# A two-layer mixer block on Trainium2: the feed-forward part in two phases, with seven half-size products in place of eight on the way up

## The chip, the cores and the metric

The kernel runs on one core of one Trainium2 chip. The figure is the device time of one execution in microseconds (us); the median of 3 runs of the kernel before is 4048.8 us (4048.6 to 4054.81). All work is done by five engines with instruction queues of their own: TensorE (PE, the matmuls; PEld is its loading of weights), VectorE (DVE), ScalarE (ACT), GpSimd (POOL) and SyncE (SP), which here issues every DMA. Each queue is worked off in order: an instruction that waits holds up all that stand behind it.

## The reference

Two layers work on 1024 tokens `x` and 256 context tokens `ctx` of 1024 channels. Each layer has three mixers side by side (a recurrent one, a gated delta rule, a Fourier one), an output projection, and then the part that the change touches:

```python
def sq_relu_mlp(h, w1, w2):
    a = jax.nn.relu(h @ w1)
    return (a * a) @ w2

for l in range(DEPTH):
    ...
    xl = xl + m[:, 2] * yx
    hx = modulate(rmsnorm(xl, norm2_g[l]), m[:, 3], m[:, 4])
    xl = xl + m[:, 5] * sq_relu_mlp(hx, mlp_w1[l], mlp_w2[l])
    # the same for the context, except in the last layer
```

`w1` is 1024 x 4096 and `w2` is 4096 x 1024, all in float32. A final norm follows.

## The kernel before, in words

Channels lie on the partitions (8 blocks of 128), tokens along the free axis. The tokens are in three pieces: A and B with 512 tokens each, and C with the 256 of the context. C is worked in layer 0 only. The residual stream of a piece is `xr`, kept in SBUF.

Every float32 product is made of three: an operand is split into a rounded high part and a low part that is the rest, and `mm3` (L293) adds high by high, high by low and low by high. ACT makes the high part of a weight (L249), POOL subtracts to get the low part (`wsplit`, L276, L289). Each matmul takes 128 input channels to 128 output channels for 512 tokens (256 for C).

The feed-forward part (`mlp`, L1491) goes through the 4096 inner channels in 16 passes of two blocks of 128. In a pass the upward product of each block takes 8 input blocks, so 24 matmuls for each of A, C and B; ACT makes the squared relu and its high part, DVE the low part (L1507). These stay in SBUF (`mhA`, `mhB`, `mhC`) and go at once into the downward product: for each of 8 output blocks, 6 matmuls (2 inner blocks by 3) and then one addition into `xr` on DVE (`residual`, L1481, L1485). A pass of layer 1 thus has 96 upward and 96 downward matmuls.

Ahead of it, at the end of `mixers` (L1740 to L1752), the output projection adds into `xr`, `rstat` (L480) gets the inverse norm of each token, and `norm` (L507) makes the high and low parts `xh` and `xl` of the normalised, modulated tokens: `spread` (L256) brings the inverse norm to all partitions by four 128 x 128 PE transposes, DVE multiplies (L526), ACT adds the shift and rounds, and DVE (L533) or POOL (L530) subtracts. This is done for A and C while PE is busy with the output projection of B; the norm of B comes last, while PE multiplies A and C.

Eight PSUM banks take the products: six for this part (ring `d`), two for small things. While layer 0's feed-forward part runs, `mod_part` streams 24 MB of `w_mod` for layer 1 and reduces it on ACT, DVE (L457) and POOL (L460). The framework lays out each engine's queue ahead of time: instructions of different steps stand interleaved where their inputs were expected to be ready.

## Time and profile before

| what | value |
|---|---|
| median of 3 runs | 4048.8 us |
| the profiled execution, its own time | 4053.91 us |
| its span, from the first to the last instruction | 4052.1 us |
| mean granted TensorE clock | 0.913 of full speed |
| PE busy | 3665.3 us (90%) |
| DVE, ACT, POOL busy | 57%, 35%, 29% |
| feed-forward part of layer 0 on PE | 1322 to about 2230 us |
| feed-forward part of layer 1 on PE | 3324 to about 4030 us |
| DMA over the span | 421.93 MB, mean 104 GB/s |

How to read it: the shares are means over stages with different limits, so the rows below are taken from the two feed-forward stages and from their starts. A matmul's recorded duration overlaps that of the next; what one costs in a full stream is the stretch of time over the number of matmuls in it. The chain of waits puts 55% of the span on the line of the matmuls (L252).

### The profile page before, as it was taken

The page shows a single profiled execution, that of the slowest core. Times are in us where ns is not written, and L with a number is a line of the kernel's source. Part 1 is how long each engine was busy: PE and PEld are TensorE (multiplying, and loading weights), DVE is VectorE, ACT ScalarE, POOL GpSimd, SP SyncE. Part 2 cuts the span into 40 slices and gives each one's busy share as a digit, 9 for nine tenths or more (in the row PEclk, how much of TensorE's full clock was granted, in tenths as well). Part 3 has the DMA queues.
Part 4 walks back from the last instruction along what each step waited for, and adds up shares of the span by engine and source line. Part 5 has one row for each costly group of instructions (what it writes and reads, how often), then busy time and mean ns, then how long its engine had stood idle before and what let it go on. Part 6 is the DMA issues. An engine that isn't in the chain of part 4 may idle for free.

```text
span 4052.1 us, 60608 instructions
## 1 busy us (share of the span) xinstructions
PE 3665.3 (90%) x24030; PEld 3077.3 (76%) x24030; DVE 2321.2 (57%) x3872; ACT 1405.0 (35%) x2571; POOL 1162.0 (29%) x870
## 2 busy tenths in 40 slices
PE   7998996886788999999999889987698889999999
PEld 5776885775677888888888766876687678888887
DVE  5646877888764544443444555658878653333334
ACT  5433443333334432222223433333333333222222
POOL 1323444332225323122111332114233233222221
PEclk8998887877888999999999899987788899999999
DMA  6334336542464212222122233246254441111111
GB/s 217 116 125 143 114 109 186 151 144 90 123 205 114 71 55 71 63 73 77 59 68 79 69 130 132 76 136 179 87 154 136 136 120 55 45 49 53 45 48 63
DMA packets 441726, 421.93 MB, mean 104 GB/s; under 512 B 28502, under 2 KB 351586, under 8 KB 441442
## 3 DMA queue, kind: packets, MB, share of 16 engines
q1 hardware_dynamic: 441442, 418.05, 33.6%
q8 instruction: 189, 3.10, 0.3%
q14 instruction: 95, 0.78, 0.1%
HBM read 324.20 MB, written 93.75 MB: 103 GB/s over the span
## 4 chain that ended last, share of the span: by engine, by line
PE 56%; DVE 8%; DMA 3%; issue 2%; ACT 2%; POOL 2%; SPq 0%; DVEq 0%; POOLq 0%; ACTq 0%
PE bank L252 55%; DMA wmod<-in_w_mod_dram 1%; DVE iD L785 1%; DVE iE L786 1%; DMA yin<-y 1%; DVE iD L779 1%; POOL wlo L289 1%; SPq L259 0%; PE bank L1145 0%; DVE macc L457 0%; PE bank L256 0%; POOL ras L1103 0%; DVE nt L272 0%; ACT whi L249 0%; DMA rvr<-rv 0%
## 5 line engine op out<-in xcount | busy, mean ns | idle before, releaser
L289 POOL TENSOR_TENSOR wlo<-wraw,whi 128x512 fp32r<-128x512 f32 x472 | 626.2, 1348 | 1731.3 <-ACT whi L249 825.7
L249 ACT ACTIVATE whi<-wraw 128x512 fp32r<-128x512 f32 x472 | 287.4, 625 | 639.4 <-PE bank L252 391.3
L252 PE MATMUL bank<-xhA,whi 128*128 128x512 f32 (+1 forms) x928 | 378.4, 408 | 0.0
L252 PE MATMUL bank<-xhB,whi 128*128 128x512 f32 (+1 forms) x928 | 365.1, 394 | 12.4 <-ACT ru L249 12.1
L252 PE MATMUL bank<-xlA,whi 128*128 128x512 f32 (+1 forms) x928 | 374.3, 404 | 1.3 <-POOL xlA L530 1.0
L252 PE MATMUL bank<-xhA,wlo 128*128 128x512 f32 (+1 forms) x928 | 372.3, 402 | 1.5 <-POOL wlo L289 1.5
L252 PE MATMUL bank<-xlB,whi 128*128 128x512 f32 (+1 forms) x928 | 365.2, 394 | 1.8 <-POOL xlB L530 1.8
L252 PE MATMUL bank<-xhB,wlo 128*128 128x512 f32 (+1 forms) x928 | 364.1, 392 | 0.0
L1485 DVE SCALAR_TENSOR_TENSOR xrB<-bank,mod,xrB 128x512 f32<-128x512 f32 x272 | 203.6, 749 | 197.2 <-PE bank L252 197.2
L252 PE MATMUL bank<-mhB,whi 128*128 128x512 f32 x1024 | 316.1, 390 | 0.0
L252 PE MATMUL bank<-mhA,whi 128*128 128x512 f32 x1024 | 315.2, 389 | 0.0
L249 ACT ACTIVATE mt<-bank 128x512 f32<-128x512 f32 (+1 forms) x160 | 88.1, 551 | 531.9 <-PE bank L252 498.0
L1485 DVE SCALAR_TENSOR_TENSOR xrA<-bank,mod,xrA 128x512 f32<-128x512 f32 x272 | 196.8, 746 | 120.3 <-PE bank L252 119.9
L252 PEld LDWEIGHTS bank<-mhA,whi 128*128 128x128 f32 x1024 | 192.2, 188 | 39.8
L252 PEld LDWEIGHTS bank<-mhB,whi 128*128 128x128 f32 x1024 | 191.1, 188 | 38.7
L252 PEld LDWEIGHTS bank<-xhA,whi 128*128 128x128 f32 (+1 forms) x928 | 179.0, 193 | 43.9 <-issue 6.2
L252 PEld LDWEIGHTS bank<-xhB,whi 128*128 128x128 f32 (+1 forms) x928 | 174.8, 188 | 49.4 <-ACT ru L249 12.5
L252 PEld LDWEIGHTS bank<-xhA,wlo 128*128 128x128 f32 (+1 forms) x928 | 178.7, 193 | 43.9 <-POOL wlo L289 2.4
L252 PEld LDWEIGHTS bank<-xlA,whi 128*128 128x128 f32 (+1 forms) x928 | 179.2, 193 | 42.8 <-POOL xlA L530 2.9
L1507 DVE TENSOR_TENSOR mhA<-mt,mhA 128x512 fp32r<-128x512 f32 x64 | 53.7, 839 | 274.7 <-ACT mt L249 274.6
L457 DVE SCALAR_TENSOR_TENSOR macc<-wmod,cs,macc 128x512 f32<-128x512 f32 x140 | 124.3, 888 | 140.9 <-DMA wmod<-in_w_mod_dram 94.4
L252 PEld LDWEIGHTS bank<-xhB,wlo 128*128 128x128 f32 (+1 forms) x928 | 174.5, 188 | 38.9 <-issue 0.3
(450 smaller groups left out, 8276.0 us busy)
## 6 DMA issues: line engine op xcount, KB each, us to landing
wraw<-in_mlp_w_dram SPq DMA_DIRECT2D x256, 256.0 KB
wmod<-in_w_mod_dram SPq DMA_DIRECT2D x192, 256.0 KB
wraw<-in_w_in_dram SPq DMA_DIRECT2D x100, 256.0 KB
wraw<-in_w_out_dram SPq DMA_DIRECT2D x80, 256.0 KB
rk<-rkb SPq DMA_DIRECT2D x16, 640.0 KB
rt<-rkt SPq DMA_DIRECT2D x16, 640.0 KB
rkb<-rk SPq DMA_DIRECT2D x40, 256.0 KB
ge<-gr SPq DMA_DIRECT2D x40, 256.0 KB
```

Source lines behind the costliest of these rows:

```text
L249: return self.S.activation(out, in_, func, **kw)
L252: return self.nc.tensor.matmul(out, lhsT, rhs, start=start, stop=stop)
L289: self.P.tensor_tensor(lo[:, o + i:o + i + m], raw, h.bitcast(F32), SUB)
L457: V.scalar_tensor_tensor(acc[:, 0], raw, c[0], acc[:, 0], MUL, ADD)
L779: (V.tensor_copy if d else self.act)(lane(D, 3 * d, i, 4), lg[d][q[i], :, q[i]])
L785: V.tensor_tensor(t, F[:, m:, j:m].to_broadcast([128, n, m]), E[:, j:m, :m].to_broadcast([128, n, m]), MUL)
L786: V.tensor_tensor(E[:, m:, :m], E[:, m:, :m], t, SUB)
L1485: self.V.scalar_tensor_tensor(x, ps, self.lv[self.l]["m"][:, mo + b, i:i + 1], x, MUL, ADD)
L1507: V.tensor_tensor(h[:, 1], t[:, :n], h[:, 0].bitcast(F32), SUB)
```

## The change

In each layer the feed-forward part now has two phases.

Up: for each pair of inner blocks (16 pairs) the product for tokens A and B is a 2 x 2 block product: two inner blocks (rows 1 and 2), two halves of the input channels, two pieces of tokens. In place of eight half-size products of 12 matmuls each there are seven, of sums: with weights A11, A12, A21, A22 and tokens B11, B21 (piece A, the two halves) and B12, B22 (piece B), S1 = A21 + A22, S2 = S1 - A11, S3 = A11 - A21, S4 = A12 - S2, and T1 = B12 - B11, T2 = B22 - T1, T3 = B22 - B12, T4 = B21 - T2. The products are A11 B11, A12 B21, S1 T1, S2 T2, S3 T3, S4 B22 and A22 T4, and seven additions on DVE put the four results together. C keeps its plain products, 48 matmuls a pair. `up_parts` makes the weight sums on DVE and splits seven of them (eight with A21, which C needs) on ACT and POOL. `norm_sums` replaces the norm of B and makes the T sums; it needs the normalised tokens of A in full, which `norm` now leaves in `keep`. The squared relu is stored to DRAM in full precision.

Down: `down_parts` loads the inner channels and `w2` back, splits them, and multiplies in groups of four inner blocks (six groups) and then of two (four groups), with one addition into `xr` for each output block and group. `xr` itself is stored to DRAM (`save_x`) ahead of the up phase and loaded back (`back_x`) ahead of the down phase. The stream of `w_mod` is spread over both phases.

The diff, cut to its core (removed lines of the old `mlp` loop are left out):

```diff
...
+                if keep:
+                    self.act(o, o, AF.Identity, bias=sh)
+                    V.tensor_tensor(self.block(xl, b), o, h.bitcast(F32), SUB)
+                else:
+                    V.scalar_tensor_tensor(self.block(xl, b), o, sh, h.bitcast(F32), ADD, SUB)
+            if not keep:
+                self.free(o)
+
+    def norm_sums(self, l, keep):
+
+        V, L = self.V, self.lv[l]
+        g, r = L["g2"], self.rs["B"]
+        rb = self.ps()
+        for j in range(4):
+            self.spread(rb[:, j * 128:j * 128 + 128], r[:, j:j + 1])
+        for j in range(2):
+            ts = {nm: (self.slot(f"{nm}h", (2, 512), F32R, "a"), self.slot(f"{nm}l", (2, 512), F32R, "a"))
+                  for nm in ("T2", "T1", "T3", "B22", "T4")}
+            for k in (2 * j, 2 * j + 1):
+                o = [self.slot("nt", (512,), kind="r") for _ in range(4)]
+                a0, a1 = self.block(keep, k), self.block(keep, k + 4)
+
+                def put(nm, x, e):
+                    h, w = (t[:, k % 2] for t in ts[nm])
+                    self.act(h, x)
+                    e.tensor_tensor(w, x, h.bitcast(F32), SUB)
+
+                for i, b in enumerate((k, k + 4)):
+                    V.scalar_tensor_tensor(o[i], self.block(self.xr["B"], b), g[:, b, 0:1], rb, MUL, MUL)
+                    self.act(o[i], o[i], AF.Identity, bias=L["m"][:, 24 + b, 0:1])
+                V.tensor_tensor(o[2], o[0], a0, SUB)
+                V.tensor_tensor(o[3], o[1], o[2], SUB)
+                put("T2", o[3], V)
+                put("T1", o[2], self.P)
+                V.tensor_tensor(o[0], o[1], o[0], SUB)
+                put("T3", o[0], self.P)
+                put("B22", o[1], self.P)
+                V.tensor_tensor(o[3], a1, o[3], SUB)
+                put("T4", o[3], V)
+                self.free(*o)
+            for nm, t in ts.items():
+                self.xs.setdefault(nm, []).append(t)
+            self.free(keep[j], keep[2 + j], self.xr["B"][j], self.xr["B"][2 + j])
...
+    def up_parts(self, l, n, x, last):
+        V = self.V
+        (a11, a12), (a21, a22) = self.raw
+        flat = lambda t: t.rearrange("p k c -> p (k c)")
+        def put(nm, w):
+            t = x[nm] = self.slot(f"u{nm}", (2, 4, 128), F32R, "a")
+            t = t.rearrange("p s k c -> p s (k c)")
+            self.act(t[:, 0], w)
+            self.P.tensor_tensor(t[:, 1], w, t[:, 0].bitcast(F32), SUB)
+        put("A11", flat(a11))
+        yield
+        s = self.slot("us", (2, 512), kind="a")
+        V.tensor_tensor(s[:, 0], flat(a21), flat(a22), ADD)
+        V.tensor_tensor(s[:, 1], s[:, 0], flat(a11), SUB)
+        put("S2", s[:, 1])
+        yield
+        put("A12", flat(a12))
+        z = self.slot("us", (2, 512), kind="a")
+        V.tensor_tensor(z[:, 0], flat(a11), flat(a21), SUB)
+        V.tensor_tensor(z[:, 1], flat(a12), s[:, 1], SUB)
+        self.free(a11, a12)
+        if n < 15:
+            self.raw[0] = self.up_load(l, 2 * n + 2)
+        yield
+        put("S1", s[:, 0])
+        self.free(s)
+        yield
+        put("S3", z[:, 0])
+        yield
+        put("S4", z[:, 1])
+        self.free(z)
+        yield
+        put("A22", flat(a22))
+        if not last:
+            put("A21", flat(a21))
+        self.free(a21, a22)
+        if n < 15:
+            self.raw[1] = self.up_load(l, 2 * n + 3)
+        yield
+    def up(self, l, last, mod, begin, end):
+        V = self.V
+        part = self.part
+        def keep(t, n, i, c):
+            self.store(self.dram(f"h{l}{n}", (128, 2, T))[:, i, c:c + t.shape[1]], t)
+        def first(ps, n, i, c):
...
+        def total(out, ps, s):
+            V.tensor_tensor(out, ps, s, ADD)
+            return out
+        def second(t, n, i, c):
+            V.scalar_tensor_tensor(t, t, 0.0, t, ALU.max, MUL)
+            keep(t, n, i, c)
+            self.free(t)
...
+        for n in range(16):
+            x, nx = part, {}
+            self.part = part = nx
+            nxt = self.up_parts(l, n + 1, nx, last) if n < 15 else end
+            cs = []
+            def prod(w, o):
+                ps = self.ps("d")
+                for k in range(4):
+                    rh, rl = xs[o][k // 2]
+                    self.mm3(ps, x[w][:, 0, k], x[w][:, 1, k], rh[:, k % 2], rl[:, k % 2], k == 0, k == 3)
+                if n == 15:
+                    for t in xs.pop(o):
+                        self.free(*t)
+                return ps
+            def ctx(i, w, h):
+                if not last:
+                    if len(cs) == i:
+                        cs.append(self.ps("d")[:, :256])
+                    for k in range(4):
+                        rh, rl = self.xrhs(4 * h + k, "C")
+                        self.mm3(cs[i], x[w][:, 0, k], x[w][:, 1, k], rh, rl, (h == 0) == (i == 0) and k == 0, (h == 1) == (i == 0) and k == 3)
+            def done(w):
+                self.free(x[w])
+                if n == 0 and w == "A11":
+                    begin()
+                next(nxt, None)
+                if n == 15:
+                    next(nxt, None)
+            tile = lambda: self.slot("ms", (512,), kind="r")
+            s1 = tile()
+            ps = prod("A11", "B11")
+            ctx(0, "A11", 0)
+            self.act(s1, ps)
+            done("A11")
+            ps = prod("S2", "T2")
+            done("S2")
+            u2 = total(tile(), ps, s1)
+            ps = prod("A12", "B21")
+            ctx(0, "A12", 1)
+            third(total(s1, ps, s1), n, 0, 0)
+            if not last:
+                first(cs[0], n, 0, 1024)
+            done("A12")
+            next(mod, None)
+            u4 = total(tile(), prod("S1", "T1"), u2)
+            done("S1")
+            ps = prod("S3", "T3")
+            t = total(tile(), ps, u4)
+            total(u2, ps, u2)
+            second(t, n, 1, 512)
+            done("S3")
+            second(total(u4, prod("S4", "B22"), u4), n, 0, 512)
+            done("S4")
+            next(mod, None)
+            ps = prod("A22", "T4")
+            if not last:
+                ctx(1, "A22", 1)
+                ctx(1, "A21", 0)
+                self.free(x["A21"])
+            done("A22")
+            second(total(u2, ps, u2), n, 1, 0)
+            if not last:
+                first(cs[1], n, 1, 1024)
+        self.free_x()
+    def down_parts(self, l, fbs, x, pieces, kh="a", kw="aaaa"):
...
+        def tokens(p, i):
+            if p == "C":
+                if i % 2:
+                    return
+                t = self.slot("mhC", (2, 2, 256), F32R, kh)
+                src = h(fbs[i])[:, :, 1024:1280]
+                x["h"][p] += [t[:, :, 0], t[:, :, 1]]
+            else:
+                t = self.slot(f"mh{p}", (2, 512), F32R, kh)
+                src = h(fbs[i])[:, fbs[i] % 2, 512 * (p == "B"):512 * (p == "B") + 512]
+                x["h"][p].append(t)
+            raw = self.slot("hraw", t.shape[2:], F32, "r")
+            self.load(raw, src)
+            self.act(t[:, 0], raw)
+            self.V.tensor_tensor(t[:, 1], raw, t[:, 0].bitcast(F32), SUB)
+            self.free(raw)
+        for i in range(len(fbs)):
+            tokens("A", i)
+            yield
+            weights(i)
+            yield
+        for p in pieces[1:]:
+            for i in range(len(fbs)):
+                if p != "C" or i % 2 == 0:
+                    tokens(p, i)
+                    yield
     def mlp(self, l, last):
...
+        groups = [list(range(i, i + 4)) for i in range(0, 24, 4)] + [[i, i + 1] for i in range(24, 32, 2)]
+        xs = [{} for _ in groups]
+        def parts(i):
+            if i == len(groups):
+                return iter(())
+            if i == len(groups) - 1:
+                return self.down_parts(l, groups[i], xs[i], pieces, "u", ("w!", "u"))
+            return self.down_parts(l, groups[i], xs[i], pieces, "x" if i == len(groups) - 2 else "a")
+        def begin():
+            self.norm_sums(l, self.kept)
+            for _ in self.pair:
+                pass
+        self.up(l, last, mod, begin, parts(0))
+        for p in pieces:
+            self.back_x(f"xm{l}", p)
+        for i, (fbs, x) in enumerate(zip(groups, xs)):
+            nxt = parts(i + 1)
             def down(p, b0=0, b1=8):
                 for b in range(b0, b1):
                     ps = self.ps("d")[:, :LEN[p]]
+                    for j, (hi, lo) in enumerate(x["w"]):
+                        h = x["h"][p][j]
+                        self.mm3(ps, hi[:, b, :], lo[:, b, :], h[:, 0], h[:, 1], j == 0, j == len(fbs) - 1)
                     self.residual(b, 40)(ps, p)
...
-        self.layout(3, r=10)
+        self.layout(3, r=12)
         self.rstat("A")
         self.gains(l, 2)
-        self.norm(l, 2, "A")
+        self.kept = [self.slot(f"keep{j}", (2, 512)) for j in range(4)]
+        self.norm(l, 2, "A", self.kept)
+        self.save_x(f"xm{l}", "A")
         if not last:
             self.rstat("C")
             self.norm(l, 2, "C")
+            self.save_x(f"xm{l}", "C")
         self.at(1.2)
         self.outproj(l, "B", yb)
         self.at(1.6)
         self.share = "uw"
-        self.first = [self.wsplit(self.w1(l, fb)) for fb in range(2)]
+        self.raw = [self.up_load(l, fb) for fb in range(2)]
+        self.part = {}
+        self.pair = self.up_parts(l, 0, self.part, last)
+        for _ in range(4):
+            next(self.pair)
+        self.save_x(f"xm{l}", "B", False)
         self.rstat("B")
-        self.norm(l, 2, "B")
         self.share = ""
         self.set_rings(d=6, m=2)
+        xh, xl = self.xh.pop("A"), self.xl.pop("A")
+        self.xs = {nm: [(xh[i], xl[i]) for i in ij] for nm, ij in (("B11", (0, 1)), ("B21", (2, 3)))}
```

What the new order looks like at three places. First PE, at the start of layer 1's feed-forward part, before (`xhA` and `xhB` are pieces A and B, `whi` and `wlo` a block of w1, the 128x128 x4 row is the `spread` for B):

```order
L252 MATMUL bank1_68<-xhA1_25204,whi_25541 128x512
L256 MATMUL bank7_74<-cst_63,rst4_3_231 128x128 x4
L252 MATMUL bank1_68<-xlA1_25208,whi_25541 128x512
...
L252 MATMUL bank1_68<-xhA3_25206,wlo_25542 128x512
L252 MATMUL bank2_69<-xhB0_25584,whi_25531 128x512
L252 MATMUL bank2_69<-xlB0_25588,whi_25531 128x512
```

and now (`uA12`, `uS1`, `uS2` and `uA22` are split weight sums, T1, T2 and T4 split token sums):

```order
L254 MATMUL bank2_69<-xhA3_25660,uA12_26003 128x512
L258 MATMUL bank6_73<-cst_63,rst4_3_231 128x128 x4
L254 MATMUL bank3_70<-T1h_26077,uS1_26013 128x512
L254 MATMUL bank3_70<-T1l_26078,uS1_26013 128x512
L254 MATMUL bank1_68<-T2h_26075,uS2_26000 128x512
...
L254 MATMUL bank0_67<-T4h_26137,uA22_26189 128x512
L254 MATMUL bank1_68<-xhA0_25657,uA11_26196 128x512
...
L254 MATMUL bank0_67<-T4l_26138,uA22_26189 128x512
L254 MATMUL bank5_72<-B22h_26081,uS4_26186 128x512
```

Before, 17 matmuls on A stood behind the `spread` and ahead of the first on B; now the products on T stand right behind it, and what is left of A is one product of the next pair.

Second, DVE at the same place, before (`nt` is a normalised block of B, `xlB` its low part):

```order
L526 SCALAR_TENSOR_TENSOR nt_25596<-xrB0_25125,g2_1_133,bank7_74 128x512
L526 SCALAR_TENSOR_TENSOR nt_25600<-xrB0_25125,g2_1_133,bank7_74 128x512
L526 SCALAR_TENSOR_TENSOR nt_25605<-xrB1_25126,g2_1_133,bank7_74 128x512
L533 SCALAR_TENSOR_TENSOR xlB0_25588<-nt_25596,mod_1_117,xhB0_25584 128x512
L526 SCALAR_TENSOR_TENSOR nt_25609<-xrB1_25126,g2_1_133,bank7_74 128x512
L533 SCALAR_TENSOR_TENSOR xlB1_25589<-nt_25605,mod_1_117,xhB1_25585 128x512
```

and now:

```order
L563 SCALAR_TENSOR_TENSOR nt_26107<-xrB0_25575,g2_1_133,bank6_73 128x512
L565 TENSOR_TENSOR nt_26087<-nt_26085,keep0_25653 128x512
L563 SCALAR_TENSOR_TENSOR nt_26108<-xrB2_25577,g2_1_133,bank6_73 128x512
L566 TENSOR_TENSOR nt_26088<-nt_26086,nt_26087 128x512
L569 TENSOR_TENSOR nt_26085<-nt_26086,nt_26085 128x512
L565 TENSOR_TENSOR nt_26109<-nt_26107,keep0_25653 128x512
L560 TENSOR_TENSOR T2l_26076<-nt_26088,T2h_26075 128x512
...
L572 TENSOR_TENSOR nt_26164<-keep3_25656,nt_26164 128x512
L1611 TENSOR_TENSOR ms_26217<-bank1_68,ms_26057 128x512
L1571 TENSOR_TENSOR us_26239<-wraw_26009,wraw_26192 128x512
L560 TENSOR_TENSOR T4l_26138<-nt_26164,T4h_26137 128x512
```

From the first L563 row to the last T4l row there are 36 instructions now (35 in layer 0), where 12 made the norm of B before.

Third, DVE at the turn from up to down in layer 1, now (`ms` are the results of the last pair, `mhA` and `mhB` the inner channels loaded back, `hraw` what lands from DRAM):

```order
L1718 TENSOR_TENSOR mhB_28455<-hraw_28456,mhB_28455 128x512
L1718 TENSOR_TENSOR mhA_28508<-hraw_28509,mhA_28508 128x512
L1611 TENSOR_TENSOR ms_28420<-bank1_68,ms_28379 128x512
L1611 TENSOR_TENSOR ms_28345<-bank1_68,ms_28345 128x512
L1615 SCALAR_TENSOR_TENSOR ms_28420<-ms_28420 128x512
L1718 TENSOR_TENSOR mhA_28549<-hraw_28550,mhA_28549 128x512
```

Splits of loaded tokens, of the second group too (the two `mhA`), stand among the additions of the last pair. Before, nothing on DVE in this part waited for a load except the stream of `w_mod`.

## Rows read from the trace of the kernel before

**Rows 1.** The page, busy time, share of the span and instructions of each engine.

```profile
PE 3665.3 (90%) x24030; PEld 3077.3 (76%) x24030; DVE 2321.2 (57%) x3872; ACT 1405.0 (35%) x2571; POOL 1162.0 (29%) x870
```

**Rows 2.** Busy time by windows, inside the two feed-forward stages.

```profile
core 0: us, PE busy (x) PEld busy (x) DVE busy (x) ACT busy (x) POOL busy (x), PEclk, DMA share, GB/s
1345.00:2215.00 870.00, 867.26 (x4580) 749.10 (x4579) 375.04 (x569) 251.70 (x451) 204.67 (x154) 1.00 0.23 69
3350.00:4000.00 650.00, 650.00 (x2869) 538.22 (x2868) 226.85 (x300) 170.65 (x299) 154.29 (x121) 1.00 0.16 49
3400.00:3600.00 200.00, 200.00 (x884) 165.58 (x884) 72.30 (x96) 49.14 (x88) 45.76 (x36) 1.00 0.15 47
```

**Rows 3.** PE in order of time, start of layer 0's stage: start us, us, instruction.

```profile
1322.33 0.27 PE L377 MATMUL bank<-cst,vraw 128*128 128x128 f32 x1
...
1336.00 0.28 PE L252 MATMUL bank<-xhC,whi 128*128 128x256 f32 x1
1336.11 0.28 PE L252 MATMUL bank<-xlC,whi 128*128 128x256 f32 x1
...
1341.75 0.40 PE L252 MATMUL bank<-xhB,whi 128*128 128x512 f32 x1
```

**Rows 4.** Busy time by windows, at the two starts.

```profile
1323.00:1345.00 22.00, 22.00 (x130) 18.98 (x129) 17.96 (x48) 14.40 (x29) 5.45 (x4) 1.00 0.10 30
3340.00:3350.00 10.00, 7.90 (x33) 5.55 (x32) 6.85 (x8) 7.93 (x14) 6.90 (x6) 1.00 0.09 28
```

**Rows 5.** PE in order of time, start of layer 1's stage.

```profile
3323.61 0.39 PE L252 MATMUL bank<-yh,wlo 128*128 128x512 f32 x1
...
3328.53 1.95 PE L252 MATMUL bank<-cst,sq 128*128 128x1 f32 x16
...
3335.29 0.65 PE L256 MATMUL bank<-cst,rst 128*128 128x128 f32 x4 [2.15 <-DVE rst L274]
```

**Rows 6.** DVE by line and shape, whole span: busy us, mean ns | idle before.

```profile
L526 DVE SCALAR_TENSOR_TENSOR nt<-xrB,g,bank 128x512 f32<-128x512 f32 x32 | 22.3, 737 | 1.0 <-PE bank L256 1.0
L533 DVE SCALAR_TENSOR_TENSOR xlB<-nt,mod,xhB 128x512 fp32r<-128x512 f32 x16 | 17.7, 1105 | 0.9 <-ACT xhB L249 0.4
```

**Rows 7.** By line and shape, 1345 to 2215 us.

```profile
L289 POOL TENSOR_TENSOR wlo<-wraw,whi 128x512 fp32r<-128x512 f32 x126 | 165.1, 1338 | 577.9 <-PE bank L252 286.1 <-ACT whi L249 244.0 <-issue 47.9
...
L457 DVE SCALAR_TENSOR_TENSOR macc<-wmod,cs,macc 128x512 f32<-128x512 f32 x84 | 71.4, 850 | 109.1 <-DMA wmod<-in_w_mod_dram 86.9 <-ACT macc L249 17.5 <-PE bank L252 3.8
...
L460 POOL TENSOR_TENSOR macc<-macc,wmod 128x512 f32<-128x512 f32 x28 | 39.9, 1423 | 66.0 <-ACT wmod L249 65.3
...
L1507 DVE TENSOR_TENSOR mhA<-mt,mhA 128x512 fp32r<-128x512 f32 x30 | 20.8, 693 | 112.2 <-ACT mt L249 112.1
```

**Rows 8.** DVE in order of time, at both starts.

```profile
1332.65 2.06 DVE L526 SCALAR_TENSOR_TENSOR nt<-xrB,g,bank 128x512 f32<-128x512 f32 x3
...
3336.06 2.06 DVE L526 SCALAR_TENSOR_TENSOR nt<-xrB,g,bank 128x512 f32<-128x512 f32 x3 [0.22 <-PE bank L256]
...
3339.54 1.34 DVE L533 SCALAR_TENSOR_TENSOR xlB<-nt,mod,xhB 128x512 fp32r<-128x512 f32 x1
...
3345.16 1.40 DVE L533 SCALAR_TENSOR_TENSOR xlB<-nt,mod,xhB 128x512 fp32r<-128x512 f32 x1
```

**Rows 9.** The instructions on xlB: duration ns min/median/max.

```profile
L533 DVE SCALAR_TENSOR_TENSOR xlB<-nt,mod,xhB x16: 737/1250/1771, 88.4 to 3345.2; 128x512 fp32r<-128x512 f32 x16
L530 POOL TENSOR_TENSOR xlB<-nt,xhB x16: 1268/1294/1782, 89.3 to 3347.6; 128x512 fp32r<-128x512 f32 x16
```

**Rows 10.** The instructions on xhA.

```profile
L249 ACT ACTIVATE xhA<-nt x16: 613/630/635, 74.2 to 3298.8; 128x512 fp32r<-128x512 f32 x16
```

**Rows 11.** PE in order of time, at the spread for A in layer 1.

```profile
3285.27 1.12 PE L256 MATMUL bank<-cst,rst 128*128 128x128 f32 x4 [4.68 <-DVE rst L274]
```

**Rows 12.** Busy time by windows, behind that wait, and the stretch before it.

```profile
3285.20:3289.50 4.30, 4.23 (x12) 3.57 (x13) 3.09 (x6) 2.26 (x4) 0.17 (x1) 0.50 0.22 64
3240.00:3290.00 50.00, 42.07 (x216) 33.81 (x216) 32.75 (x56) 17.08 (x23) 15.57 (x11) 0.93 0.73 211
```

More of the change, by code (lines that the diff above doesn't have):

```diff
@@ L505, in rstat, with norm @@
         self.rs[p] = r
-    def norm(self, l, which, p):
+    def norm(self, l, which, p, keep=None):
         V = self.V
@@ L1489, in w1, with up_load @@
         return self.A["mlp_w1"][l].rearrange("(k p) c -> p k c", p=128)[:, :, fb * 128:fb * 128 + 128]
+    def up_load(self, l, fb):
+        ts = [self.slot("wraw", (4, 128), kind="r") for _ in range(2)]
+        for h, t in enumerate(ts):
+            self.load(t, self.w1(l, fb)[:, h * 4:h * 4 + 4])
+        return ts
+    def up_parts(self, l, n, x, last):
[37 more added lines that the diff above has]
+        yield
@@ L1549, in mlp @@
                 self.norm(l + 1, 1, "C")
-            for w in ws:
+            for _ in nxt:
+                pass
+            for w in x["w"]:
                 self.free(*w)
-            for _ in range((fb + 2) * 8 // 5 - fb * 8 // 5):
-                next(mod, None)
+        for _ in mod:
+            pass
         if not last:
@@ L1558, in mlp @@
             self.norm(l + 1, 1, "B")
-        for h in hs.values():
-            self.free(*(h if isinstance(h, list) else [h]))
     def final(self):
```

85 lines of the change are left out of this document (45 added, 40 removed).

## The prediction, made before the changed kernel was run

> **What bounds the kernel now.** I read the page's busy shares first, then busy time by windows over the two feed-forward stages, then PE and DVE in order of time at the starts of these stages, and last DVE and POOL grouped by line and shape for the durations.
>
> PE is busy 90% of the span [rows 1], and in the feed-forward stages it is the only limit: 867.3 of 870 us in layer 0 and 650.0 of 650 us in layer 1, at a granted clock of 1.00, with DVE busy for 43% and 35%, POOL for 24% of each, and DMA moving 69 and 49 GB/s [rows 2]. A matmul of 512 columns costs there 200 us / 884 = 0.2262 us [rows 2], one of 256 columns 0.12 us [rows 3]. So a matmul taken out of these stages shortens the kernel by its full price, if the others can follow.
>
> **The matmuls.** Up, a pair of inner blocks has 96 matmuls of 512 columns for A and B; seven products of 12 make 84. Down and C stay as they are in number. 12 fewer x 16 pairs x 2 layers = 384, x 0.2262 = **86.9 us off the path**.
>
> **The start of the up phase.** This is what I price highest against it. Before, in layer 0, PE had 48 matmuls of A and 48 of C to do while the norm of B was made; it reached B at 1341.75 without a wait [rows 3], and was busy for 22.00 of 22 us [rows 4]. In layer 1 it lost 2.15 us at the `spread` [rows 5] and 10 - 7.90 = 2.1 us behind it [rows 4], together 4.25 us. Now only 24 matmuls on A stand ahead of the T products (and 24 short ones of C in layer 0), and the T sums are three times the DVE work.
>
> DVE's queue in layer 1, from the first multiplication to the low part of the last T4, holds 36 instructions: 8 like the old L526, at 0.737 us [rows 6] 5.9 us; one addition from a bank, some 0.7; and 27 with both inputs in SBUF. For these the trace has two prices: 0.693 us alone [rows 7], and 1.34 and 1.40 for L533 rows that lie beside POOL's subtractions [rows 8]; the mean of the 16 L533 rows on B, the same place and neighbours, is 1.105 us [rows 6]. POOL will have 16 of its own there, at 1.294 us (the middle one of [rows 9]) 20.7 us, so I take the mean: 27 x 1.105 = 29.8. Sum 36.4 us (25.3 with 0.693; with every shared pair in turn, 5.9 + 0.7 + 27 x 0.693 + 20.7 = 46.0). ACT has 28 roundings and shifts there, at 0.630 us [rows 10] some 18 us, inside this.
>
> Layer 1: the multiplications start at 3336.06 as before [rows 8], since the sums of squares ahead of them are unchanged; the last T4 is there at 3336.1 + 36.4 + 0.5 for its last matmuls = 3373.0. PE without a wait would need from 3323.8 (behind the last matmul of the projection, [rows 5]): 24 x 0.2262 = 5.4, sums of squares 1.95 and spread 0.65 [rows 5], the other 60 matmuls 13.6, and 12 of the next pair that stand ahead of the last T4 rows 2.7: 24.3, so 3348.2. Lost 24.8, before 4.25: **20.6 us more**.
>
> Layer 0: one instruction fewer, 35.3 us from 1332.65 [rows 8]; done at 1368.5. PE's own work from 1322.4 (behind two transposes, [rows 3]): 5.4 + 24 x 0.12 + 1.95 + 0.65 + 13.6 = 24.5, so 1346.9. Lost 21.5, before nothing: **21.5 us more**.
>
> The Trainium skill has a rule that speaks against the mean I took: SBUF — State Buffer, section "Who interferes with whom", says that a VectorE instruction with two SBUF inputs and a GpSimd instruction that reads SBUF exclude each other for their whole length. The L533 rows agree with it: 0.737 at the least, 1.250 in the middle, 1.771 at the most [rows 9]. By it the 27 and POOL's 16 add up to 18.7 + 20.7 = 39.4 us with the bank-reading ones beside them, 3.0 more than I take, and the sum below would come out at some 4018 us.
>
> **The clock.** After an idle of 4.68 us [rows 11] PE ran for 4.3 us at a granted clock of 0.50, which is 1.2 of 2.4 GHz [rows 12]. The T products come in drips, so I expect the half clock there; while DVE is late it costs nothing, and behind the last T4 about half of 4.3 us: 2 us a layer, **4 us** (0 to 8).
>
> **The steady up phase.** A pair takes PE 84 x 0.2262 = 19.0 us, and 48 x 0.12 = 5.8 more in layer 0. POOL has 7 splits (8 in layer 0): 8 x 1.338 = 10.7 us, and for the first 8 pairs of layer 0 3.5 additions of `w_mod` at 1.423, 5.0 [rows 7]. DVE has there 7 additions from banks, 7 instructions with two SBUF inputs at 0.693 and 3.5 of `w_mod` at 0.850 [rows 7]: those in SBUF 7.8 us. Even if POOL and these never overlap, 10.7 + 5.0 + 7.8 = 23.5 is under 24.8. I take 0. With 1.105 for the 7 it is 26.4, 1.6 x 8 = 13 us: the upper end. Below nothing there is no room, since PE has no idle left to give back. Six banks let DVE be late by six products.
>
> **The turn and the down phase.** For the first down product, four blocks of `w2` (8 splits on POOL, 10.4 us) and of inner channels must be ready. Their buffers come free product by product in the last pair, the last after 4 x 2.7 = 10.9 of its 19.0 us; four splits are then still ahead, 5.2 us, and that fits. But about 8.4 MB (first group 4.2, `xr` 4.2) and the last pairs' own 2.1 MB each cross DMA in that time, and DVE's additions stand behind splits that wait for these loads. At 211 GB/s, the most that a window of these stages' neighbourhood shows [rows 12], 12.6 MB take 60 us against two pairs (38) and six banks (16): 6 us late. That row has the DMA engines at 0.73, not full, so it may be 0. I take 2 a layer, **4 us** (0 to 12). In the down phase a group of four blocks brings 4.2 MB in 43.5 us of PE time, 97 GB/s; its splits are as many as before, and DVE has fewer additions into `xr` (10 rounds in place of 16). The four more ACT instructions in the norm of A lie beside the projection of B.
>
> **Sum.** -86.9 + 20.6 + 21.5 + 4 + 4 = -36.8 us. The profiled execution took 4053.9, so 4017.1; the median of the runs is 5.1 lower, and 4048.8 - 36.8 = **4012 us**.
>
> **Rivals.**
> *A, the start is cheap.* Speaks for it: 0.693 us for the same subtraction where POOL is idle; against it: POOL has 20.7 us of work there. With DVE at 25.3 and 24.6 us, the losses are 9.5 and 10.8, the turn costs nothing: -86.9 + 9.5 + 10.8 + 4 = -62.6, 3986 us.
> *B, the trip through DRAM becomes the bound: slower.* Its place is the down phase, where inner channels and `w2` now both come by DMA: 33.6 MB in layer 1 for 1536 x 0.2262 = 347 us of PE, 37.8 MB in layer 0 for 347 + 768 x 0.12 = 439 us. It decides below 97 GB/s and turns the sign at 33.6 / (347 + 36.8) = 88 GB/s; at 80 GB/s it costs 73 + 33 us, 4118 us. For it: 69 GB/s is all that these stages move today. Against it: that is what they ask for; 211 GB/s in [rows 12].
> *C, all upper ends.* POOL and DVE strictly in turn at the start (+9.6 a layer), the turn at 6 a layer, 13 us in layer 0's early pairs: -36.8 + 19 + 8 + 13 = +3, 4052 us. For it: the 1.771 us of [rows 9].
>
> **How the numbers follow.** Forecast 62% (3996 to 4032), A 18%, C 12% (4032 to 4056), B 8%. No change I call within 0.2%, 8.1 us, which is about what a measurement of this kernel can tell: that is the upper half of C, 6%. Slower: B and a point of C, 9%; faster 85%. The range leaves out the lowest quarter of A, the upper half of C, and B: 3978 to 4044 us.
>
> **What would show it.** The page: some 380 fewer matmuls of 512 columns, DMA up by about 94 MB (inner channels 21.0 and 16.8, `xr` 5.2 and 4.2, each there and back). By windows: PE full at clock 1.00 in both phases, with one dent of 20 to 25 us at each start, PE waiting there for DVE's T low parts, and DVE without idle. If the dent is under 12 us, A holds; if `mhA` or `wlo` waiting for DMA holds PE up all through the down phase, B. The forecast is wrong if PE's matmuls of 512 columns are spaced by more than 0.23 us in the middle of either phase.

## The result, and the profile after

The changed kernel takes 4074.7 us (median of 5 runs, 4066.4 to 4077.2) against 4048.8 us (5 runs, 4042.8 to 4054.8): a ratio of 1.0056, 95% interval 1.0039 to 1.0074 (estimated from all runs; the two medians alone give 1.0064). It is slower, where 4012 us was forecast. Its profiled execution took 4074.69 us, its span 4072.9.

The page of the changed kernel, against [rows 1], with the line on DMA:

```profile
PE 3616.7 (89%) x23646; PEld 3022.0 (74%) x23646; DVE 2600.5 (64%) x4104; ACT 1397.0 (34%) x2547; POOL 1410.7 (35%) x998
...
DMA packets 502727, 516.37 MB, mean 127 GB/s; under 512 B 34198, under 2 KB 375714, under 8 KB 502434
```

The 384 matmuls are gone (24030 to 23646), and with them only 49 of the 86.9 us of busy time, while the span grew by 21. To find the stretch, I took the start of the last matmul of the projection of B (`yh`), of the first down product (`mhA`) and of the last one (`mhB`) from PE's answers by tile; here those of layer 0 of the changed kernel (duration ns min/median/max, first and last start in us):

```profile
L254 PE MATMUL bank<-yh,wlo x162: 280/389/796, 1199.6 to 1315.3; 128*128 128x512 f32 x98, 128*128 128x256 f32 x64
...
L254 PE MATMUL bank<-mhA,whi x512: 387/389/486, 1812.5 to 2239.6; 128*128 128x512 f32 x171
...
L254 PE MATMUL bank<-mhB,wlo x256: 389/389/476, 1846.3 to 2260.8; 128*128 128x512 f32 x128
```

The differences of such starts, for all kernels of this study (us; "up" from the end of the projection to the first down product, "down" from there to the last one; the mixers between the two feed-forward parts took 1083 to 1108 us in all of them, with the same work, and are not read for causes):

```
                              up 0   down 0  both 0 | up 1   down 1  both 1 | run / before
before                          -       -     907.8 |   -       -     706.1 | 1
after                         497.2   448.3   945.5 | 339.4   349.8   689.2 | 1.0056
e1  w_mod in the down phase   432.5   475.9   908.4 | 340.9   349.8   690.7 | 0.9972
e2  ones-matmuls later        442.7   449.6   892.3 | 342.2   349.8   692.0 | 0.9935
e3  loads earlier             500.8   455.0   955.8 | 340.9   349.8   690.7 | 1.0088
e8  stores later              488.6   448.4   937.0 | 340.8   349.8   690.6 | 1.0045
e9  loads left out            449.9   448.3   898.2 | 340.9   349.8   690.7 | 0.9938
e5  eight products            476.4   448.3   924.7 | 352.2   349.7   701.9 | 1.0041
e10 eight products, later     454.9   449.6   904.5 | 352.0   349.8   701.8 | 0.9997
e4  lows on VectorE           497.4   448.3   945.7 | 332.8   349.7   682.5 | 1.0051
e4b lows on GpSimd            508.1   448.2   956.3 | 339.4   349.8   689.2 | 1.0088
e6  e2 and slices             433.5   451.1   884.6 | 334.4   350.0   684.4 | 0.9900
e11 e6 and lows on VectorE    431.5   450.5   882.0 | 327.4   353.2   680.6 | 0.9885
```

Layer 1 went as forecast (706.1 - 43.5 + 24.6 = 687.2; measured 689.2). Layer 0 was forecast at 907.8 - 43.5 + 25.5 = 889.8 and took 945.5: nearly all of the miss is there, and by the table in its up phase. Busy time by windows, in the upward phase (first two), the downward phase and the upward phase of layer 1:

```profile
core 0: us, PE busy (x) PEld busy (x) DVE busy (x) ACT busy (x) POOL busy (x), PEclk, DMA share, GB/s
1400.00:1600.00 200.00, 181.81 (x923) 156.78 (x924) 97.31 (x121) 69.47 (x126) 107.40 (x76) 0.92 0.35 114
1600.00:1800.00 200.00, 194.00 (x1013) 166.44 (x1011) 107.87 (x133) 68.51 (x126) 85.84 (x62) 0.98 0.45 144
1880.00:2180.00 300.00, 300.00 (x1589) 259.78 (x1588) 156.81 (x224) 56.51 (x97) 61.13 (x40) 1.00 0.31 100
3410.00:3640.00 230.00, 228.59 (x1007) 189.14 (x1008) 140.01 (x179) 72.09 (x125) 137.99 (x90) 1.00 0.35 114
```

Of these four only the two of layer 0's upward phase have PE below full clock and idle for more than 1.5 us; DVE and POOL are busy for about half of them. What PE waits for there (who waited for whom, 1400 to 1880 us: total us, times, longest):

```profile
PE bank L254 <- DVE macc L459: 26.0, 8, 7.4
PE bank L254 <- POOL macc L462: 6.0, 4, 2.1
```

`macc` is no part of the change. It is the sum that `mod_part` makes of `w_mod` for layer 1, and the instructions that wait are its `128x1` matmuls with the ones (the ones-matmuls from here on). PE in order of time at the longest of these waits:

```profile
1402.82 0.59 PE L254 MATMUL bank<-cst,macc 128*128 128x1 f32 x2 [7.38 <-DVE macc L459]
1403.27 0.78 PE L254 MATMUL bank<-T4l,uA 128*128 128x512 f32 x1
1403.84 1.05 PE L254 MATMUL bank<-T4h,uA 128*128 128x512 f32 x2
...
1407.06 3.15 PE L254 MATMUL bank<-cst,macc 128*128 128x1 f32 x14 [0.46 <-POOL macc L462]
```

The products on T4 behind them needed nothing from `macc`, but they stand behind them in PE's queue and ran only after the wait. In the kernel before, the ones-matmuls came 13 to 15 us after the last addition into `macc`; here one of the three groups between 1400 and 1560 us, on DVE, POOL and PE:

```profile
1418.87 0.75 DVE L457 SCALAR_TENSOR_TENSOR macc<-wmod,cs,macc 128x512 f32<-128x512 f32 x1 [3.60 <-DMA wmod<-in_w_mod_dram]
1420.57 1.29 POOL L460 TENSOR_TENSOR macc<-macc,wmod 128x512 f32<-128x512 f32 x1 [5.46 <-ACT wmod L249]
1435.66 1.84 PE L252 MATMUL bank<-cst,macc 128*128 128x1 f32 x16
```

In the changed kernel, DVE just before the 7.38 us wait, in order of time, and SP's queue of DMAs:

```profile
1391.88 1.28 DVE L1611 TENSOR_TENSOR ms<-bank,ms 128x512 f32<-128x512 f32 x2
1396.15 1.29 DVE L1611 TENSOR_TENSOR ms<-bank,ms 128x512 f32<-128x512 f32 x2 [2.99 <-DMA h<-ms]
...
1401.22 1.54 DVE L459 SCALAR_TENSOR_TENSOR macc<-wmod,cs,macc 128x512 f32<-128x512 f32 x2 [3.19 <-DMA wmod<-in_w_mod_dram]
```

```profile
1393.92 0.33 SPq L264 DMA_DIRECT2D h<-ms  x1
1395.02 0.33 SPq L264 DMA_DIRECT2D h<-mt  x1
1396.08 0.38 SPq L261 DMA_DIRECT2D wraw<-in_mlp_w_dram  x1
1398.33 0.33 SPq L261 DMA_DIRECT2D wmod<-in_w_mod_dram  x1
```

SP's own waits between 1385 and 1403 us (L264 are stores, L261 loads; two of five rows):

```profile
SPq L264 <- ACT mt L251: 5.0, 2, 4.3
...
SPq L261 <- DMA h<-mt: 1.9, 1, 1.9
```

The load of `wmod` leaves at 1398.33, behind stores of inner channels that waited 5.0 us for their results, and after 1.9 us of its own for its buffer, which an earlier store had still to leave. DVE gets it 2.9 us later. The price of such a wait is not the 7.38 us alone (windows behind it):

```profile
1403.00:1407.00 4.00, 3.60 (x9) 2.40 (x9) 1.60 (x2) 1.50 (x3) 4.00 (x4) 0.50 0.17 66
1407.00:1412.00 5.00, 4.94 (x22) 4.84 (x23) 1.75 (x4) 0.00 (x0) 1.23 (x2) 0.50 0.18 52
1412.00:1420.00 8.00, 8.00 (x46) 7.42 (x46) 1.22 (x3) 2.44 (x5) 2.58 (x2) 0.84 0.36 115
```

The granted clock is 0.50, 1.2 of 2.4 GHz, for 9 us and 0.84 for 8 more: some 4.5 + 1.3 = 6 us lost again. Over the phase 32 us of waits and about 20 us at the lower clock (200 x 0.08 + 200 x 0.02 by the windows) make up most of the 55.7 (945.5 - 889.8) that were not forecast.

The starts in the changed kernel, against [rows 4, 8]: windows over the chain of VectorE, and its first and last instruction in each layer.

```profile
1326.00:1367.00 41.00, 23.05 (x63) 13.17 (x62) 39.63 (x36) 21.86 (x37) 29.96 (x19) 0.63 0.12 35
3370.00:3411.00 41.00, 25.62 (x55) 13.07 (x53) 40.46 (x37) 22.41 (x37) 30.42 (x19) 0.63 0.11 32
```

```profile
1327.10 2.06 DVE L563 SCALAR_TENSOR_TENSOR nt<-xrB,g,bank 128x512 f32<-128x512 f32 x3 [2.17 <-PE bank L258]
...
1365.16 1.66 DVE L560 TENSOR_TENSOR T4l<-nt,T4h 128x512 fp32r<-128x512 f32 x1
...
3370.54 2.06 DVE L563 SCALAR_TENSOR_TENSOR nt<-xrB,g,bank 128x512 f32<-128x512 f32 x3 [0.82 <-PE bank L258]
...
3408.96 1.76 DVE L560 TENSOR_TENSOR T4l<-nt,T4h 128x512 fp32r<-128x512 f32 x1
```

The chains take 39.7 and 40.2 us (forecast 35.3 and 36.4), with DVE busy 97% and 99% of the windows. DVE and POOL side by side, and a subtraction of DVE while POOL was idle:

```profile
1333.04 1.76 DVE L565 TENSOR_TENSOR nt<-nt,keep 128x512 f32<-128x512 f32 x1
1334.22 1.71 POOL L560 TENSOR_TENSOR T3l<-nt,T3h 128x512 fp32r<-128x512 f32 x1
1334.73 1.75 DVE L560 TENSOR_TENSOR T2l<-nt,T2h 128x512 fp32r<-128x512 f32 x1
1335.89 1.72 POOL L560 TENSOR_TENSOR T1l<-nt,T1h 128x512 fp32r<-128x512 f32 x1
...
1342.10 0.68 DVE L560 TENSOR_TENSOR T4l<-nt,T4h 128x512 fp32r<-128x512 f32 x1
```

### The profile page after: what moved, and what is told of

It reads as the page before. It is cut to its first block, busy times and chain, and to the rows that moved or that the text cites. A ratio compares the mean times of both kernels' runs of the same rounds, so it can differ in the third digit from the quotient of the medians.

```text
span 4072.9 us, 61291 instructions
## 1 busy us (share of the span) xinstructions
PE 3616.7 (89%) x23646; PEld 3022.0 (74%) x23646; DVE 2600.5 (64%) x4104; ACT 1397.0 (34%) x2547; POOL 1410.7 (35%) x998
## 5 line engine op out<-in xcount | busy, mean ns | idle before, releaser
L1560 POOL TENSOR_TENSOR uS<-us,uS 128x512 fp32r<-128x512 f32 x128 | 198.8, 1563 | 134.9 <-ACT uS L251 116.9
L1560 POOL TENSOR_TENSOR uA<-wraw,uA 128x512 fp32r<-128x512 f32 x112 | 158.9, 1426 | 189.1 <-ACT uA L251 189.1
L254 PE MATMUL bank<-mhB,wlo 128*128 128x512 f32 x512 | 199.3, 389 | 0.0
L254 PE MATMUL bank<-mhA,wlo 128*128 128x512 f32 x512 | 199.2, 389 | 0.0
L254 PE MATMUL bank<-xhB,whi 128*128 128x512 f32 (+1 forms) x416 | 165.4, 398 | 13.9 <-ACT ru L251 13.9
L254 PE MATMUL bank<-xhA,whi 128*128 128x512 f32 (+1 forms) x416 | 177.0, 427 | 0.2 <-ACT whi L251 0.2
L254 PE MATMUL bank<-xlA,whi 128*128 128x512 f32 (+1 forms) x416 | 174.5, 421 | 1.3 <-POOL xlA L532 1.0
L254 PE MATMUL bank<-xhA,wlo 128*128 128x512 f32 (+1 forms) x416 | 171.9, 414 | 1.0 <-POOL wlo L291 1.0
L254 PE MATMUL bank<-xhA,uA 128*128 128x512 f32 x512 | 169.6, 393 | 1.4 <-DVE ms L1611 1.4
L254 PE MATMUL bank<-xlB,whi 128*128 128x512 f32 (+1 forms) x416 | 165.0, 397 | 0.0
```

The source lines that it names most:

```text
L254: return self.nc.tensor.matmul(out, lhsT, rhs, start=start, stop=stop)
L1560: self.P.tensor_tensor(t[:, 1], w, t[:, 0].bitcast(F32), SUB)
```

## The experiments

Each ratio is to the kernel before, run beside it on the same chip.

**Where the 55 us go: the stream moved away (e1).**

```diff
             done("A12")
-            next(mod, None)
...
             done("S4")
-            next(mod, None)
...
                         next(nxt, None)
+                    if len(fbs) == 4 and b % 3 == 2:
+                        next(mod, None)
```

> The stream of w_mod (its loads, its sums on VectorE and GpSimd, its ones-matmuls on TensorE) is moved whole out of the upward phase of layer 0 into the downward phase. The products and all else stay. Three theories of the 55 us that the upward phase of layer 0 lost beyond its clean passes of 24.86 us. T1, the queue: the ones-matmuls stand in TensorE's in-order queue ahead of products and wait for late sums (32 us of waits) and the half clock follows each wait: with the stream gone every pass is 24.9 us, the 16 passes take 30 + 16 x 24.9 = 428 us instead of 495, the ones-matmuls' own 11 us come back in the downward phase: 4074.7 - 50 to 55 = 4020 to 4025 us. T2, too much work on VectorE and GpSimd in that phase: the same here. T3, SP's queue: the loads of w_mod stand behind stores that wait: the same here, if loads of w_mod do not meet the same in the downward phase. Rival R: TensorE loses the time for another reason (stores of inner channels, half clock from the start): the passes stay at 28 to 40 us and the time above 4060 us.

Measured 4038.1 us, ratio 0.9972 (0.9955 to 0.9988). The up phase is as all three theories had it, 432.5 us for 428, but the down phase gave 27.6 back, not 11, so the forecast of 4020 to 4025 us was missed: soon after the turn, where the loads for the down phase are under way, PE waits 11.2 us once for `macc`, and this window shows it:

```profile
1700.00:1800.00 100.00, 87.12 (x463) 76.20 (x462) 54.50 (x69) 41.70 (x73) 48.07 (x34) 0.91 0.72 236
```

**The queue or the load (e2).** The ones-matmuls and the addition behind them wait for the next call; `ones` holds them unchanged:

```diff
         for g in range(j0, j1, 4):
+            if owed:
+                ones(*owed)
+                owed = None
...
-            ps = self.ps()
-            for j in range(4):
-                for i in range(n):
-                    self.mm(ps[:, j * 2 + i:j * 2 + i + 1], acc[:, i, j * 128:j * 128 + 128], self.C("ONE"))
...
+            owed = g, n, acc
             yield
```

> The stream of w_mod stays in the upward phase with the same loads and the same sums at the same places; only its eight ones-matmuls and the addition behind them are put one step (half a pass, 12.4 us) later in program order, so that TensorE reaches them when the sum has long been done. T1 (the wait stands in TensorE's queue ahead of products that are ready): the 32 us of waits on macc and the half clock behind them go, passes of 24.9 and 27 us, 4074.7 - 40 to 55 = 4020 to 4035 us. T2 (VectorE and GpSimd have too much to do in that phase, the ones-matmuls are only the first that show it): the wait moves to the products, for their banks or their weights, passes stay at 28 to 35 us, and the time falls by less than 15 us, to 4060 us or more. T3 (loads late in SP's queue): the sums are as late as before; if they are late by less than 12.4 us it goes as T1.

Measured 4019.1 us, ratio 0.9935 (0.9912 to 0.9958). PE's waits on `macc` between 1400 and 1880 us are gone, and the phase is full with the same work on the others at a higher rate:

```profile
1400.00:1600.00 200.00, 198.73 (x1084) 172.69 (x1083) 132.85 (x148) 82.05 (x151) 131.09 (x88) 1.00 0.43 137
1600.00:1800.00 200.00, 200.00 (x1091) 174.21 (x1090) 118.83 (x149) 74.58 (x134) 87.20 (x62) 1.00 0.57 186
```

1084 matmuls in place of 923 in the first 200 us, DVE and POOL each busy for 66% of it. T2, that they have too much to do, is refuted; T1 holds. DVE still waited 39.9 us for the loads of `w_mod` between 1376 and 1760 us, but the sums were now done 4 to 7 us ahead of the ones-matmuls (three groups between 1400 and 1530 us).

**Why the sums are late (e3, e8, e9).** e3 fetches both loads of the next step at the end of each step; two slots of the ring `r` are then held across it.

```diff
-                raw = self.slot("wmod", (512,), kind="r")
-                self.load(raw, wv[:, k, g * 128:g * 128 + 512])
+                fetch(1)
+                raw = there.pop(0)
...
                 self.free(raw)
+                if early and k % 2:
+                    fetch(2)
```

> The ones-matmuls stay where they are; the two loads of w_mod of each step are issued one step (half a pass, 12.4 us) earlier in SP's queue. T3 (the sums are late because their loads stand in SP's in-order queue behind stores that wait for results): VectorE's 38 us of waits on w_mod go, the sums are in time, the waits of TensorE on macc fall from 32 to under 10 us and the time by 30 to 55 us, to 4020 to 4045 us. T1 with sums that are late because VectorE and GpSimd come to them late in their own queues: VectorE's waits on w_mod go but TensorE's on macc stay over 20 us, and the time falls by less than 15 us, to 4060 us or more.

Measured 4085.5 us, ratio 1.0088 (1.0064 to 1.0112), worse than either expected. The loads were not early: DVE (1376 to 1820 us) still waits for them, and far longer for slots of `r` that a store must leave first (11.7 us on `h<-ms` in the changed kernel).

```profile
DVE ms L1622 <- DMA h<-mt: 53.4, 12, 5.4
DVE macc L468 <- DMA wmod<-in_w_mod_dram: 43.7, 8, 8.0
```

e8 issues each store of inner channels behind the next tile (`flush` issues the store that is owed and frees its tile):

```diff
-        def keep(t, n, i, c):
-            self.store(self.dram(f"h{l}{n}", (128, 2, T))[:, i, c:c + t.shape[1]], t)
...
+        def keep(t, w, n, i, c):
+            flush()
+            owing.append((t, w, n, i, c))
```

> Ones-matmuls, sums and loads of w_mod stay where they are in program order; each store of an inner-channel tile is put behind the next such tile in SP's queue, so that SP finds it made and does not wait for VectorE's or ScalarE's result (143 us of such waits in the upward phase of layer 0). T3 (the loads of w_mod come late because SP's in-order queue stands at these stores): waits of TensorE on macc fall from 32 to under 12 us and the time by 25 to 50 us, to 4025 to 4050 us. If the loads are late for another reason (their slots of the ring r, which the stores now hold a product longer): waits on macc stay at 25 us or more, 4065 us or more.

Measured 4061.1 us, ratio 1.0045 (1.0027 to 1.0063), PE's waits on `macc` 28.7 us. The waits are where the second reading had them (25 us or more), the time lies between the two readings. It does not decide on T3: SP's waits at the stores fell only from 145 to 126 us, so the edit did not take away what it was to take away, and the waits of loads for slots that a store had still to leave grew from 15.2 to 36.5 us.

e9 removes the loads themselves (ScalarE's scaled copy goes to a tile of its own):

```diff
+        if once:
+            one = self.slot("wmod", (512,), kind="r")
+            self.load(one, wv[:, 0, j0 * 128:j0 * 128 + 512])
...
-                raw = self.slot("wmod", (512,), kind="r")
-                self.load(raw, wv[:, k, g * 128:g * 128 + 512])
+                if once:
+                    raw = one
...
```

> The changed kernel with the stream of w_mod at its old places, but its loads left out: all sums of the stream read one tile that is loaded once (so the shift and scale of layer 1, and with them the output, are not the reference's); VectorE, GpSimd, ScalarE and TensorE issue the same work. T3 (the sums are late because their loads come late through SP's queue): TensorE's 32 us of waits on macc fall under 8 us, the passes to 25 and 27 us, the time by 40 to 55 us, to 4010 to 4025 us. T1 with sums late in VectorE's and GpSimd's own queues: the waits stay at 20 us or more and the time above 4050 us.

Measured 4020.5 us, ratio 0.9938 (0.9918 to 0.9959). PE waits for nothing between 1400 and 1880 us with the ones-matmuls at their old place (one wait of 5.7 us for `macc` is left ahead of that):

```profile
1400.00:1600.00 200.00, 200.00 (x1084) 173.81 (x1084) 110.41 (x140) 78.36 (x145) 115.87 (x83) 1.00 0.28 92
```

So the sums came too late for the ones-matmuls because the loads did (that much of T3 is shown), and cost what they cost because of where the ones-matmuls stand (T1): taking away either link gives the same time. What held the loads back is open, SP's order, the twelve slots of `r` or the transfer itself: e9 removes all three, and e3 and e8 changed one of the first two at the price of the other. It is not shown either that the change made them later: DVE waited longer for them in the kernel before, in the same stretch of time (1376 to 1820 us, before and changed):

```profile
DVE macc L457 <- DMA wmod<-in_w_mod_dram: 54.0, 25, 4.4
```

```profile
DVE macc L459 <- DMA wmod<-in_w_mod_dram: 38.0, 19, 4.4
```

**The two halves of the change (e5, e10).** Two phases, with eight products (two in a bank) in place of the seven and their sums:

```diff
-            ps = prod("A11", "B11")
...
+            one, two = ("A11", "A12"), ("A21", "A22")
+            first(prod(one, ("B11", "B21")), n, 0, 0)
...
+            first(prod(two, ("B11", "B21")), n, 1, 0)
...
+            first(prod(one, ("B12", "B22")), n, 0, 512)
...
+            first(prod(two, ("B12", "B22")), n, 1, 512)
```

> One half of the change alone: the two phases with the inner channels in DRAM stay, but the upward products of A and B are again eight products of halves (96 matmuls of 512 columns a pair, both halves summed in one bank), with plain halves of B in place of the T sums and four weight parts in place of eight; evictions on ScalarE. From the prediction: the two phases cost 4 us (the turn), and the start of B costs about what it did before: 4048.8 + 4 = 4053 us, if the stream of w_mod does not hold TensorE up; against the changed kernel 86.9 us of matmuls more and 41 us less at the starts. T1: passes are 27.1 + 5.8 = 33 us and VectorE has little to do, so the sums of w_mod come in time and the 55 us do not show: 4053 us (4045 to 4062). T3 (loads behind waiting stores): stores wait for results here too, so waits on macc of 10 us or more stay: 4065 to 4090 us.

Measured 4062.3 us, ratio 1.0041 (1.0025 to 1.0057): at the edge between the two expectations, with 11.1 us of waits on `macc` in layer 0. e10 is e5 with the edit of e2.

> Two phases through DRAM with eight products, as in the earlier run (1.0041 of before), and in addition the ones-matmuls of w_mod one step later. If the 1.0041 was the ones-matmuls' wait too (11 us of waits on macc and the half clock behind them, 17 us more in the feed-forward part of layer 0 than before): that part falls from 924.7 to 906 to 910 us, the ratio to 0.999 to 1.001: the trip through DRAM costs nothing, and what the seven products give is the difference to the run with seven products and later ones (0.9935). If the trip itself costs: the ratio stays at 1.002 or more.

Measured 4044.4 us, ratio 0.9997 (0.9979 to 1.0016); the feed-forward part of layer 0 took 904.5 us. The trip through DRAM costs nothing that can be measured; what cost was, here too, `macc`. Between e10 and e2 stands what seven products in place of eight give: 904.5 - 892.3 = 12.2 and 701.8 - 692.0 = 9.8 us of 43.5 in each layer. The rest, 31 and 34 us, is lost at the starts: by an estimate with each matmul at its price in a full stream, PE lost 30.6 us of the first 60.5 behind the projection in layer 0 and 34.8 of the first 69.5 in layer 1 in e2, and 1.2 and 1.8 us in e10.

**The starts (e4, e4b, e6, e11).** e4 turns `self.P` into `V` for the low parts of T1, T3 and B22 (12 instructions a layer), e4b `V` into `self.P` for T2 and T4 (8):

```diff
-                put("T1", o[2], self.P)
+                put("T1", o[2], V)
...
```

> At the start of the upward phase the 12 low parts of T1, T3 and B22 go from GpSimd to VectorE; nothing else. The chain on VectorE from the first multiplication to the low part of the last T4 took 40.2 us in layer 1 and 39.7 in layer 0. X, the two engines take turns one for one when both read SBUF: 12 x (1.27 - 0.69) = 7.0 us a layer less, the chain 33 to 36 us, the time 8 to 14 us lower than the changed kernel's 4074.7. Y, VectorE's own queue with a price of its own (1.1 us an instruction) sets the chain: 12 instructions more at 0.69 to 1.1 us: the chain 46 to 53 us, the time 15 to 25 us higher.

> The opposite move: the 8 low parts of T2 and T4 go from VectorE to GpSimd; nothing else. X (the engines take turns one for one): GpSimd's part of the start is 24 instructions at 1.27 to 1.72 us, the chain up to the low part of the last T4 43 to 48 us in place of 40, the time 6 to 16 us above the changed kernel's 4074.7. Y (VectorE's own queue sets it): 8 instructions at 1.1 us fewer there, the chain 31 to 33 us, the time 12 to 18 us lower.

e4: 4065.5 us, ratio 1.0051 (1.0035 to 1.0066). The chains take 34.8 us (1330.56 to 1365.40) and 32.7 (3364.52 to 3397.26), so the price is X's; layer 1 is 6.7 us shorter, layer 0 not at all, where PE still waits 32.1 us for `macc`. The gain in time cannot be told from none. e4b: 4078.7 us, ratio 1.0088 (1.0066 to 1.0110). Its chains take 38.2 and 38.7 us, which neither theory gave: 24 instructions at 1.72 us on POOL would be 41. Layer 1 stayed as it was; why layer 0 lost 10.8 us was not followed up.

e6 adds to e2 a first pair in slices, with all its weight parts split before the norm of B:

```diff
-        for _ in range(4):
+        for _ in range(7):
             next(self.pair)
...
+                bs = [self.ps("d") for _ in jobs]
+                for k in range(4):
+                    for ps, (w, o) in zip(bs, jobs):
+                        rh, rl = xs[o][k // 2]
+                        self.mm3(ps, x[w][:, 0, k], x[w][:, 1, k], rh[:, k % 2], rl[:, k % 2], k == 0, k == 3)
```

> The ones-matmuls one step later as in the earlier run (4019 us), and the start of B changed: all weight parts of the first pair are split before the norm of B begins, both products of A come first, and the five products on T2, T1, T3, B22 and T4 of the first pair are run in five banks slice by slice, three matmuls on each as the slice of its T is there. If TensorE waits at the start for VectorE's whole chain and then has 13.6 us of products left (T, the start): 45 of these 60 matmuls, 10.2 us a layer, lie beside the chain, and the chain is shorter by the four splits of weights on GpSimd that stood in it (4 x 1.3 = 5 us): the up phases 8 to 15 us shorter in each layer, 3995 to 4005 us. Rival: the chain of VectorE goes on into the second pair's weights and the gain of the start is lost there: within 6 us of 4019.

Measured 4001.6 us, ratio 0.9900 (0.9882 to 0.9919): the up phases are 9.2 and 7.8 us shorter than in e2, the chains 34.6 and 35.3 us. Last, e11, the edits of e6 and e4 together:

> The version with ones later and the first pair in slices (0.990 of before), and the 12 low parts of T1, T3 and B22 on VectorE in place of GpSimd. With GpSimd's four splits of weights gone from the chain, the chain is 35 us there. X (turns one for one): the 12 exchanged for cheaper ones, but VectorE's 39 instructions with two SBUF inputs at 0.69 and 9 others at 0.74 are then 33.5 us without any partner: 0 to 2 us a layer less, the ratio 0.989 to 0.990. Y (1.1 us an instruction on VectorE whatever GpSimd does): 13 us a layer more, 0.996.

Measured 3998.2 us (3991.2 to 4004.5), ratio 0.9885 (0.9859 to 0.9910), the lowest here, though its interval overlaps that of e6. Its chains of VectorE:

```profile
1333.45 2.06 DVE L574 SCALAR_TENSOR_TENSOR nt<-xrB,g,bank 128x512 f32<-128x512 f32 x3 [2.18 <-PE bank L258]
...
1363.36 0.68 DVE L571 TENSOR_TENSOR T4l<-nt,T4h 128x512 fp32r<-128x512 f32 x1
...
3307.05 2.06 DVE L574 SCALAR_TENSOR_TENSOR nt<-xrB,g,bank 128x512 f32<-128x512 f32 x3 [1.27 <-PE bank L258]
...
3336.93 0.68 DVE L571 TENSOR_TENSOR T4l<-nt,T4h 128x512 fp32r<-128x512 f32 x1
```

30.6 us each, 4 to 5 us less than e6, where X gave 0 to 2: the 48 instructions of that chain come at 0.64 us each, closer than their own 0.68 and 0.74. Y is refuted.

## Why the prediction was wrong

1. **The matmuls, right.** 384 fewer; where PE does not wait, 442 or 443 matmuls in each 100 us of layer 1's stretch as before ([rows 2]: 884 in 200).
2. **The steady up phase, "I take 0", the step that failed.** It added up rates: 23.5 us of DVE and POOL against 24.8 of PE. The rates were right, as e2 shows with PE full. What I left out is a wait that is no rate: the ones-matmuls stand in PE's own queue, and the sum that they need hangs on loads. Before, the ones-matmuls found their sums ready, 13 to 15 us after the last addition, and PE had no wait on `macc` in 1376 to 1820 us, although DVE waited for the loads then too. The change gave the steps of the stream new places, and PE now reaches the ones-matmuls before the sum is done; I priced the stream by its work and gave its place in PE's queue no term. It cost 53 us by e2 (945.5 - 892.3) and 47 by e9 (945.5 - 898.2), in layer 0.
3. **The starts, right in kind, too small.** I took the mean of the L533 rows, 1.105 us, and got chains of 35.3 and 36.4 us; they took 39.7 and 40.2. PE lost 30.6 us at the start of layer 0 and 31.8 at that of layer 1 (reckoned as for e10, over the first 60.5 and 69.5 us), where I had 23.5 and 26.8 with the clock. This was the smaller part of the miss. That layer 1 still came out within 2 us is partly luck: the 2 us of its turn were not needed, and the kernel before had lost 5.8 us there, not 4.25.
   The Trainium skill's rule (SBUF — State Buffer, "Who interferes with whom") gave 39.4, and the trace agrees with it in kind: beside POOL a subtraction of DVE takes 1.75 us, alone 0.68, and POOL's goes from 1.27 (the least in [rows 9]) to 1.72. That its sum comes so near is partly luck: two of DVE's beside POOL start 1.69 us apart (1333.04 and 1334.73), less than the 0.68 + 1.27 = 1.95 us of two that exclude each other in full, and the bank-reading ones, which that sum took as hidden, stand in DVE's chain.
4. **The clock, too small.** 2 us a layer was for the starts, where it was hidden or nearly so. Behind the waits of step 2 it cost about 20 us in layer 0.
5. **The turn and the down phase, right.** The first `mhA` came without a wait in both layers, at full clock, and the down phases took 448.3 and 349.8 us. Rival B, the DRAM bound, is refuted by PE busy for 300.00 of 300 us at 100 GB/s in the down phase, and by e10.
6. **The rivals.** C came nearest, 4052 us, but not in cause: its 13 us in layer 0's early pairs were VectorE and GpSimd in turns, not a queue. A is refuted by the chains.

With the one wait taken away (e2) the ratio is 0.9935 (0.9912 to 0.9958); the forecast of 4012 / 4048.8 = 0.9909 lies just outside. The feed-forward parts are then 892.3 and 692.0 us for 889.8 and 687.2.

## What to carry to other kernels

When a change moves the work around a side product, follow that product to the end: from its loads to the sum that needs them, and to the instruction that waits for this sum at the head of PE's queue, even if that work has nothing to do with the change. Look at the distance between the end of the sum and that instruction, in the kernel before and in the new order. Small matmuls on a side product belong one step later than the step that completes it: here this alone took the ratio from 1.0056 to 0.9935. Rates that fit say that an engine can follow, not that each instruction is there when the queue reaches it.

## What the runs showed of the hardware

A wait of 7.38 us on PE was followed by 9 us at a granted clock of 0.50 and 8 us at 0.84, so it cost nearly twice its length. VectorE and GpSimd with operands in SBUF slowed each other to 1.75 and 1.72 us, from 0.68 and 1.27, and took turns every 1.7 us; with 12 of GpSimd's subtractions given to VectorE (e4) VectorE's chain became shorter, by 4.9 and 7.5 us, though it had 12 instructions more.
